# Row normalisation of a 1024 x 4096 array on one core: loads moved from the SyncE queue to the ScalarE queue

## The chip, the core and the metric

The kernel runs on one core of a Trainium2 chip. The metric is the device time of one execution in microseconds (us); lower is better. The kernel before takes 84.19 us, the median of 4 runs (84.07 to 84.33). The profile shown below was taken from one further execution, which took 84.27 us; the hardware profiler's span in it, from the first to the last instruction, is 82.5 us, so 1.8 us lie around the span.

## The reference

Each of the 1024 rows of a float32 array with 4096 columns is divided by its own length:

```python
norm = np.sqrt(np.sum(x ** 2, axis=axis, keepdims=True) + eps)
return (x / norm).astype(np.float32)
```

The axis is the last one, eps is 1e-12. 16.78 MB are read and as many are written; for every element there is one square, one addition and one multiplication.

## The kernel before, in words

The 1024 rows are cut into four tiles. A tile is 128 partitions x 2 rows (R = 2) x 4096 columns of float32; a partition holds two neighbouring rows, which are 32 KB in one piece both in memory and on the chip, and a tile is 4 MiB. The pool `io` has four buffers, as many as there are tiles, so each tile `xt` has a place of its own and no load ever waits for a buffer.

The first loop (L44 to L47) issues all four loads, one transfer per tile, with `nc.sync.dma_start` (L46): they stand in the instruction queue of SyncE (SP), one after the other, and nothing is waited for between them.

The second loop (L49 to L73) works through the tiles in order. For each tile:

- ScalarE (ACT) runs Square over the first and then the second row of every partition (L53), 128 x 4096 elements each, and accumulates the sums of squares into a column of `ssq`. The squares themselves go to one scratch tile `sq`. Each Square is followed by a short read of the accumulator. The first Square needs a table load, which stands at the head of ScalarE's instructions.
- ScalarE takes the root of the two sums plus eps (L61). The first time this needs another table load.
- VectorE (DVE) takes the reciprocal (L67) and multiplies the two rows by it, in place (L70).
- SyncE issues the store of the tile (L73), again one transfer of 4 MiB. It waits until VectorE is done with the tile.

So SyncE's instructions before are: four loads without waits, then four stores, each with its wait. Both kinds of transfer go through one queue, and a store's data stand behind those of every load that was issued before it. ScalarE issues no transfers. TensorE does nothing and GpSimd (POOL) only sets four constants. At the end (L104) every engine is drained and SyncE waits until the last store has landed.

Of the kernel before, what the change touches and what calls it, by code (L numbers as in the profile page):

```python
# [1 line left out]

# [4 lines left out]


@with_exitstack  # L10
def kernel(
    ctx: ExitStack,
    tc: tile.TileContext,
    x: bass.AP,
    axis: bass.AP,
    eps: bass.AP,
    out: bass.AP,
):
    nc = tc.nc
    P = nc.NUM_PARTITIONS  # L20

    assert isinstance(axis, int) and axis in (-1, len(x.shape) - 1)
    eps = float(eps)

    x = x.flatten_outer_dims()
    out_flat = out.flatten_outer_dims()
    N, D = x.shape
    assert N % P == 0

    R = 2  # L30
    n_tiles = N // (P * R)
    x = x.rearrange("(t p r) d -> t p (r d)", p=P, r=R)
    out_t = out_flat.rearrange("(t p r) d -> t p (r d)", p=P, r=R)

    io = ctx.enter_context(tc.tile_pool(name="io", bufs=n_tiles))
    scratch = ctx.enter_context(tc.tile_pool(name="scratch", bufs=1))
    stats = ctx.enter_context(tc.tile_pool(name="stats", bufs=4))

    sq = scratch.tile([P, D], mybir.dt.float32)
    eps_t = scratch.tile([P, 1], mybir.dt.float32)  # L40
    nc.vector.memset(eps_t, eps)  # L41

    xts = []
    for i in range(n_tiles):  # L44
        xt = io.tile([P, R, D], mybir.dt.float32)
        nc.sync.dma_start(out=xt.rearrange("p r d -> p (r d)"), in_=x[i])  # L46
        xts.append(xt)  # L47

    for i in range(n_tiles):  # L49
        xt = xts[i]  # L50
        ssq = stats.tile([P, R], mybir.dt.float32)
        for r in range(R):
            nc.scalar.activation(  # L53
                out=sq,
                in_=xt[:, r],
                func=mybir.ActivationFunctionType.Square,
                accum_out=ssq[:, r : r + 1],
            )

        rstd = stats.tile([P, R], mybir.dt.float32)  # L60
        nc.scalar.activation(  # L61
            out=rstd,
            in_=ssq,
            func=mybir.ActivationFunctionType.Sqrt,
            bias=eps_t,
        )
        nc.vector.reciprocal(out=rstd, in_=rstd)  # L67

        for r in range(R):
            nc.vector.tensor_scalar_mul(  # L70
                out=xt[:, r], in0=xt[:, r], scalar1=rstd[:, r : r + 1]
            )
        nc.sync.dma_start(out=out_t[i], in_=xt.rearrange("p r d -> p (r d)"))  # L73


# [1 line left out]
_INS = ['x', 'axis', 'eps']  # L77
_OUTS = [((1024, 4096), 'float32')]
#: Inputs that are plain numbers.
_NUMBERS = {'axis': -1, 'eps': 9.999999960041972e-13}  # L80


# [26 lines left out]
```

## Time and profile before

| What | Value |
|---|---|
| median of 4 runs | 84.19 us (84.07 to 84.33) |
| profiled execution | 84.27 us |
| its span | 82.5 us |
| DVE busy | 19.2 us (23%) |
| ACT busy | 33.4 us (41%) |
| mean traffic over the span | 407 GB/s |
| DMA packets | 1152, of which 128 under 512 B |
| share of the 16 DMA engines taken by the one queue | 96.2% |
| store issues on SP start at | 26.90, 35.33, 45.05 and 55.64 us |

How to read it: engine rows count busy time of compute instructions; instructions that only issue transfers are not counted as busy. A table by stretches gives for each stretch of the span the busy time of each engine, the number of its instructions, the granted TensorE clock, the mean busy share of the 16 DMA engines and the rate in GB/s. A packet is counted to the stretch in which it starts, so short stretches can show shares over 1. "To landing" is the time from the issue of a transfer to its last semaphore update.

### The profile page before, as it was taken

How to read it: one execution, taken by the hardware profiler on the slowest of the kernel's cores; microseconds unless marked ns; L12 is line 12 of the kernel's file. 1: busy time of each engine (PE TensorE's matmuls, PEld its weight loads, DVE VectorE, ACT ScalarE, POOL GpSimd, SP SyncE). 2: the span in 40 equal slices, each digit the busy share in tenths (PEclk: the TensorE clock that was granted, in tenths of full speed). 3: DMA queues.
4: the chain of work that ended last, by engine and by line, in shares of the span. 5: the costliest groups of instructions: out<-in, count | busy, mean ns of one | idle time of the engine just before them, and what ended most of it. 6: DMA issues, size and time to landing. Idle time of an engine off the chain costs nothing.

```text
span 82.5 us, 98 instructions
## 1 busy us (share of the span) xinstructions
DVE 19.2 (23%) x13; ACT 33.4 (41%) x22; POOL 0.2 (0%) x4
## 2 busy tenths in 40 slices
DVE  0000000000299019910498003990000000000000
ACT  6000007999699972999419996000000000000000
POOL 0000000000000000000000000000000000000000
DMA  7779997996998999899959989998998998999890
GB/s 191 302 334 445 508 429 334 508 493 302 477 508 365 397 508 445 350 477 493 270 254 508 493 350 429 509 397 365 508 445 350 477 508 350 413 508 413 350 508 0
DMA packets 1152, 33.55 MB, mean 407 GB/s; under 512 B 128, under 2 KB 128, under 8 KB 128
## 3 DMA queue, kind: packets, MB, share of 16 engines
q1 hardware_dynamic: 1152, 33.55, 96.2%
HBM read 16.78 MB, written 16.78 MB: 407 GB/s over the span
## 4 chain that ended last, share of the span: by engine, by line
DMA 50%; ACT 9%; DVE 3%; DVEq 3%; SPq 1%; issue 0%
DMA xt<-in_x_dram 50%; ACT sq L53 9%; DVE xt L70 3%; DVEq L104 3%; SPq L46 1%; ACT rstd L61 0%; DVE rstd L67 0%
## 5 line engine op out<-in xcount | busy, mean ns | idle before, releaser
L53 ACT ACTIVATE sq<-xt 128x4096 f32<-128x4096 f32 x8 | 28.9, 3617 | 16.5 <-DMA xt<-in_x_dram 16.4
L70 DVE TENSOR_SCALAR xt<-xt,rstd 128x4096 f32<-128x4096 f32 x8 | 18.5, 2350 | 0.1
L67 DVE RECIPROCAL rstd<-rstd 128x2 f32<-128x2 f32 x4 | 0.7, 166 | 35.5 <-ACT rstd L61 35.5
L53 ACT ACT_TABLE_LOAD x1 | 1.3, 1283 | 0.7 <-PEq L90 0.7
L53 ACT ACTIVATION_READ_ACCUMULATOR sq<-xt 128x1 f32 x8 | 1.5, 186 | 0.0
L61 ACT ACT_TABLE_LOAD x1 | 1.3, 1283 | 0.0
L61 ACT ACTIVATE rstd<-ssq,eps_t 128x2 f32<-128x2 f32 x4 | 1.2, 295 | 0.1
L41 DVE MEMSET eps_t<- 128x1 f32 x1 | 0.1, 59 | 0.8 <-PEq L90 0.8
L90 POOL MEMSET const-bfloat16-1.0<- 128x1 bf16 x1 | 0.1, 101 | 0.0
L90 POOL MEMSET const-uint8-127<- 128x1 uint8 x1 | 0.1, 101 | 0.0
L90 POOL MEMSET const-float32-0.0<- 128x1 f32 x1 | 0.1, 98 | 0.2 <-issue 0.2
L90 POOL MEMSET const-float32-1.0<- 128x1 f32 x1 | 0.1, 98 | 0.0
## 6 DMA issues: line engine op xcount, KB each, us to landing
xt<-in_x_dram SPq DMA_DIRECT2D x4, 4096.0 KB, 26.1
out_dram<-xt SPq DMA_DIRECT2D x4, 4096.0 KB, 26.5
```

The costliest lines, as they stand in the source:

```text
L41: nc.vector.memset(eps_t, eps)
L46: nc.sync.dma_start(out=xt.rearrange("p r d -> p (r d)"), in_=x[i])
L53: nc.scalar.activation(out=sq, in_=xt[:, r], func=mybir.ActivationFunctionType.Square, accum_out=ssq[:, r : r + 1],)
L61: nc.scalar.activation(out=rstd, in_=ssq, func=mybir.ActivationFunctionType.Sqrt, bias=eps_t,)
L67: nc.vector.reciprocal(out=rstd, in_=rstd)
L70: nc.vector.tensor_scalar_mul(out=xt[:, r], in0=xt[:, r], scalar1=rstd[:, r : r + 1])
L90: nc = _bacc.Bacc("TRN2", target_bir_lowering=False, num_devices=1)
L104: with _tile.TileContext(nc) as tc:
```

## The change

The four loads are issued with `nc.scalar.dma_start` in place of `nc.sync.dma_start`; the stores stay on SyncE. The order of the issues, the tiles and the arithmetic are the same. The pool `stats` now has `n_tiles` buffers, which is 4 as before, and the rest is names.

```diff
-    x = x.rearrange("(t p r) d -> t p (r d)", p=P, r=R)
+    x_t = x.rearrange("(t p r) d -> t p (r d)", p=P, r=R)
...
-    stats = ctx.enter_context(tc.tile_pool(name="stats", bufs=4))
+    stats = ctx.enter_context(tc.tile_pool(name="stats", bufs=n_tiles))
...
     for i in range(n_tiles):
-        xt = io.tile([P, R, D], mybir.dt.float32)
-        nc.sync.dma_start(out=xt.rearrange("p r d -> p (r d)"), in_=x[i])
+        xt = io.tile([P, R, D], F32)
+        nc.scalar.dma_start(out=xt.rearrange("p r d -> p (r d)"), in_=x_t[i])
         xts.append(xt)
```

On the engines it does this (the instruction lists of the two kernels side by side; PE, DVE and POOL are unchanged):

```
ACT: +L46 DMACopy xt<-in_x_dram 128x8192 x4     ahead of the first L53 LoadActFuncSet
SP:  -L46 DMACopy xt<-in_x_dram 128x8192 x4     ahead of the first L73 DMACopy
```

More of the change, by code (lines that the diff above doesn't have):

```diff
@@ L20 @@
     P = nc.NUM_PARTITIONS
+    F32 = mybir.dt.float32
     assert isinstance(axis, int) and axis in (-1, len(x.shape) - 1)
@@ L36 @@
     scratch = ctx.enter_context(tc.tile_pool(name="scratch", bufs=1))
-    stats = ctx.enter_context(tc.tile_pool(name="stats", bufs=4))
-    sq = scratch.tile([P, D], mybir.dt.float32)
-    eps_t = scratch.tile([P, 1], mybir.dt.float32)
+    stats = ctx.enter_context(tc.tile_pool(name="stats", bufs=n_tiles))
+    sq = scratch.tile([P, D], F32)
+    eps_t = scratch.tile([P, 1], F32)
     nc.vector.memset(eps_t, eps)
@@ L50 @@
         xt = xts[i]
-        ssq = stats.tile([P, R], mybir.dt.float32)
+        ssq = stats.tile([P, R], F32)
         for r in range(R):
@@ L58 @@
             )
-        rstd = stats.tile([P, R], mybir.dt.float32)
+        rstd = stats.tile([P, R], F32)
         nc.scalar.activation(
```

## The prediction

> **What bounds the kernel now.** I read the rows by slices first, then the table by stretches, then SP's own waits. ACT is busy 41% of the span and DVE 23%, so neither is the bound. In the table I cut the span at the moments when ACT starts on a tile (the load has just landed: 12.96, 22.68, 32.40, 42.98), and after that in stretches of 9.6 us:
>
> ```profile
> core 0: us, DVE busy (x) ACT busy (x) POOL busy (x), PEclk, DMA share, GB/s
> 0.00:2.10 2.10, 0.06 (x1) 1.28 (x1) 0.20 (x4) 1.00 0.70 187
> 2.10:12.96 10.86, 0.00 (x0) 0.00 (x0) 0.00 (x0) 1.00 0.93 398
> 12.96:22.68 9.72, 0.59 (x2) 9.00 (x7) 0.00 (x0) 1.00 1.00 432
> 22.68:32.40 9.72, 6.07 (x4) 7.71 (x6) 0.00 (x0) 1.00 1.00 432
> 32.40:42.98 10.58, 5.64 (x5) 7.71 (x5) 0.00 (x0) 1.00 1.01 396
> 42.98:52.60 9.62, 3.81 (x3) 7.71 (x5) 0.00 (x0) 1.00 1.01 436
> 52.60:62.20 9.60, 3.01 (x2) 0.00 (x0) 0.00 (x0) 1.00 1.01 437
> 62.20:71.80 9.60, 0.00 (x0) 0.00 (x0) 0.00 (x0) 1.00 1.01 437
> ```
>
> The DMA share is 0.93 to 1.01 from 2.10 on: the sixteen DMA engines are the bound, in loads (432 GB/s) as in stores (437 GB/s). One stretch stands out: the fourth load took 10.58 us where the two before it took 9.72. So 0.86 us are lost about where the loads end and the stores begin, with the engines counted as busy.
>
> The stores do not start when they are issued:
>
> ```profile
> SPq L73 <- DVE xt L70: 41.4, 4, 13.9
> SPq L104 <- DMA out_dram<-xt: 25.5, 3, 9.6
> ```
>
> ```profile
> xt<-in_x_dram SPq DMA_DIRECT2D x4, 4096.0 KB, 26.1
> out_dram<-xt SPq DMA_DIRECT2D x4, 4096.0 KB, 26.5
> ```
>
> The first store is issued at 26.90 but needs 25.7 us to land (52.6): it stands behind two loads. Singly, the four stores take 25.7, 27.0, 27.0 and 26.0 us to landing, so they land at 52.6, 62.3, 72.05 and 81.64. Each time a store is issued, other data still stand in the queue: the last one is issued at 55.64 and its turn comes only when the third is through. ACT and DVE are covered by some 15 us.
>
> **The change part by part.**
> *The issue on ACT.* Before, SP's four load issues took 1.91 us, 383 to 532 ns each, from 0.73 on. ACT's first instruction before, a table load of 1.28 us, also starts at 0.73. In the changed instruction list the four issues stand ahead of that table load, so the first load leaves at the same moment if ACT issues as fast as SP. No row shows an issue on ACT; the first one alone matters, since the engines then have 9.7 us of work. Bounds: -0.4 us (no issue time at all) to +1.28 (as late as behind the table load). I take 0, by the nearest row, SP's. The table load moves to about 2.64 and ends at 3.9; the wait for the first tile (until 12.96) hides it by 9 us. Without that cover it and the issues would cost 1.91 + 1.28 = 3.2 us. On SP the first instruction is now the wait of store 1, which stood there from 13.0 anyway; nothing else is behind the loads there. The stores keep their waits and their order, and no wait is added to an engine. `stats` had 4 buffers and has 4: nothing.
>
> *What really moves: who gets the engines from 26.9 on.* The data of both kernels are the same, 33.55 MB, and as long as the engines never run dry, the end stays where it is. So I need the time at which the last store can start, and the time at which the other seven transfers are through.
> (1) Store 1 is issued at 26.90. The first load, issued at 0.73, shows its first packets at 1.7, so I put the first store data at 27.9.
> (2) Load work left then, at the pace of 9.72 us per tile: load 3 until 32.40 and load 4 until 42.12, together 14.2 us.
> (3) Packets are all of one size (1024 of 32 KB, next to 128 small ones), and a tile of stores takes the engines as long as one of loads. No row shows two queues side by side. The stores' share lies between 0 (loads first, as now) and 1 (stores first). I take one half. The 14.2 us then become 28.4.
> (4) I keep the 0.86 us once, as a loss that is not shared: load 4 lands at 27.9 + 28.4 + 0.86 = 57.2 instead of 42.98.
> (5) From landing to store 4's issue it took 55.64 - 42.98 = 12.66 us (two Squares, the root, the reciprocal, two products, each without a gap worth naming); with 1.0 us to the first packet, store 4 can start at 57.2 + 13.7 = 70.9.
> (6) Stores 1 to 3 and all loads are done when store 3 lands, 72.05 as before. But a landing comes after its data: load 1 took 11.2 us from its first packet to its landing, 1.5 more than the pace, in which start and landing are both contained. So the engines run dry between 70.5 and 72.05.
> The 15 us of cover are used up. Taking the early end, 70.5, the engines stand empty for 0.4 us; taking the late one there is no gap at all. If the 0.86 us is doubled too, store 4 starts at 71.8 and the gap is 1.3 at most. I take **+0.3 us**, between 0 and 1.3 and near the case that counts the loss once. Stores 2 and 3 come in time: they are issued at 35.3 and, load 3 then landing at 27.9 + 2 x 4.5 = 36.9, at about 49.6, while store 1 alone lasts until 27.9 + 19.4 = 47.3 and store 2 far beyond.
>
> Sum: 84.27 (profiled) + 0 + 0.3 = 84.57. The profiled execution is 0.08 us above the median, so against the runs shown: 84.19 + 0.3 = **84.5 us**.
>
> *A rule beside the row.* The row says 432 GB/s for loads and 437 for stores, each alone. The Trainium skill, "DMA: Bandwidth & Descriptors", section "Issuing engines are not separate DMA queues", speaks against any gain: transfers issued from different engines run on the same 16 DMA engines, and only issue time is saved. By it the sum would be 84.2 or more. The same page, section "Queues, rings and completion order", has each DMA engine take turns between queues packet by packet, which would make the share one half; its section "Latency and other measured facts" lists copies with 214 GB/s per direction at full rate, which is 428 for both, and an estimate from it is 1 to 2% over some 28 us, up to 0.5 us more than my sum. No run here shows either yet.
>
> **The rivals.**
> *B, stores get more than half.* With a share s, load 4 lands at 27.9 + 14.2/(1-s) + 0.86. The gap opens when this plus 13.7 passes 70.5 to 72.05: from s = 0.49 to 0.52 on. At s = 0.55 it is 2 to 3.5 us (86 to 87.7). If stores always went first: stores 1 and 2 run until 47.3, load 3 lands at 51.8, load 4 at 62.4; store 3 can start at 65.5, 3.1 us after the engines ran dry, and store 4 at 76.1, 0.9 us after store 3: 84.2 + 4.0 = 88.2. The worst share would leave the whole 13.7 us bare (97.9). For it: the price rises at once, there is no cover left. Against: equal packets.
>
> *C, mixing costs rate.* The 0.86 us were lost where loads and stores meet. If each load packet that stands beside store packets paid a part of it, say 0.86 us per two packets: 14.2 us of loads are 14.2/(9.72/8) = 12 packets per engine, so up to 5 us: 89. Against: the stretch shows it once, and the next one is back at 436.
>
> *D, the other side: the loss at the meeting goes away.* Place: 32.40 to 42.98. Price: 0.86 us, to 83.3. If the last loads lost it because the whole stream turns from one direction to the other at one point, a stream that is mixed from 27.9 on need not turn. It decides when store 4 still starts before 70.5, that is with a share of at most one half: without the loss load 4 lands at 56.3 and store 4 can start at 70.0. For it: no other stretch lost anything. Against: mixing may as well pay it at its start.
>
> *E, the directions have limits of their own.* Then loads and stores would run side by side at full rate: load 4 still lands at about 43, store 4 is issued at 55.6 and starts at 56.7 after stores 1 to 3, and lands 10 us later, some 15 us before now: 69. Against: the share is 1.00 in one direction alone, and nothing here shows an engine doing more.
>
> *S, nothing changes*, because no engine runs dry and nothing is lost or saved: 84.2. That the change does not do what it says is out, by the instruction lists.
>
> **How the numbers follow.** About 0.2% is what a measurement of this kernel can tell from no change (84.02 to 84.36). Forecast A (a small gap, 84.4 to 85.2): 0.28. B (85.2 to 92, mostly below 88): 0.22. C (85 to 90): 0.10. D (83.0 to 84.0): 0.24. E (about 69): 0.04. S: 0.12. So slower 0.60, same 0.12, faster 0.28. The range reaches from D's low end, 83.0, to stores first, 88.2, and leaves out E and the upper parts of B and C, some 0.15. The forecast's own range is 84.4 to 85.2.
>
> **What would show it.** Step (1) to (4): ACT's start on the fourth tile, at 57 instead of 42.98; a later start, above 58.5, is B or C, and the table by stretches tells which (430 GB/s from 28 to 57 and empty slices near 70 for B; below 425 throughout for C). Step (5): store 4's issue 12.7 us after that start. Step (6): a thin slice of DMA near 70. D: no such slice, and a span near 81.6. The issue on ACT: the first tile's start at 12.96. The prediction is wrong altogether if the fourth tile still starts near 43 (loads first, or E).

## The result and the profile after

The changed kernel takes 84.45 us (median of 40 runs, 84.23 to 84.89), the kernel before in the same sessions 84.3 us (65 runs). The ratio is 1.0021, with a 95% interval of 1.0013 to 1.0029: slower by about 0.2 us. The profiled execution of the changed kernel took 84.89 us, at the upper end of its runs, with a span of 83.1 us; that of before took 84.27. The pair of profiles therefore differs by 0.6 us where the medians differ by 0.15, and only what stands out from that is read here.

First the transfers by queue, from the page of the changed kernel. There are two queues now, with half the packets each:

```profile
q10 hardware_dynamic: 576, 16.78, 49.1%
q1 hardware_dynamic: 576, 16.78, 46.8%
```

The table by stretches, cut where ScalarE starts on a tile (columns as in the prediction):

```profile
12.87:22.57 9.70, 0.58 (x2) 9.00 (x6) 0.00 (x0) 1.00 1.00 432
22.57:35.77 13.20, 8.99 (x5) 7.72 (x5) 0.00 (x0) 1.00 1.00 390
35.77:55.14 19.37, 4.78 (x3) 7.72 (x6) 0.00 (x0) 1.00 1.00 433
55.14:72.60 17.46, 4.78 (x3) 7.71 (x5) 0.00 (x0) 1.00 0.99 426
```

The reader sees three things. The first tile starts at 12.87 (12.96 before), so the issue on ScalarE costs nothing. The fourth load takes 19.37 us, twice the 9.70 of a load alone, at 433 GB/s in all: loads and stores share the engines one to one and lose no rate. And the stretch 22.57 to 35.77, in which the first store comes up, runs at 390 GB/s; against 432 that is 13.20 x (1 - 390/432) = 1.3 us lost. Before, the same reckoning for the stretch 32.40 to 42.98 at 396 GB/s gives 0.9 us.

Now around the last store, which is issued at 67.79:

```profile
66.00:69.00 3.00, 1.76 (x1) 0.00 (x0) 0.00 (x0) 1.00 0.88 382
69.00:72.00 3.00, 0.00 (x0) 0.00 (x0) 0.00 (x0) 1.00 1.14 492
72.00:75.00 3.00, 0.00 (x0) 0.00 (x0) 0.00 (x0) 1.00 0.89 382
```

Packets are counted where they start, so three neighbouring stretches scatter about 1; there is no empty one. The gap of the forecast is not there. It would be in the profile if it were: an experiment below shows how it looks.

Where the 1.3 us go can be read from one more row of the changed kernel, for the stretch from the issue of store 1 (26.80) to 30.9; the queue of the loads is q10:

```profile
DMA packets 44, 1.44 MB, mean 352 GB/s; under 512 B 0, under 2 KB 0, under 8 KB 0
## 3 DMA queue, kind: packets, MB, share of 16 engines
q10 hardware_dynamic: 44, 1.44, 103.4%
```

No store packet starts in the 4.1 us after the issue. In the next 0.4 us eight of them do. And the load packets in these 4.1 us are slow: 44 of them took 103.4% of 16 engines, 1.54 us each, where a load alone needs 16 x 9.70 / 128 = 1.21 us per packet. The kernel before has the same at the end of its fourth load, from 38.60 to 40.70, ahead of the first store packet:

```profile
DMA packets 32, 1.05 MB, mean 499 GB/s; under 512 B 0, under 2 KB 0, under 8 KB 0
q1 hardware_dynamic: 32, 1.05, 161.7%
```

That is 1.617 x 16 x 2.1 / 32 = 1.70 us each, and they are the last of the loads: up to 40.70 the queue has started 16.78 MB, all that is read. So the loss falls on the load packets just ahead of the first store packets, not on load packets that run side by side with stores.

### The profile page after: what moved, and what is told of

The parts are those of the page before. It is cut to its first block, busy times and chain, and to the rows that moved or that the text cites. A ratio compares the mean times of both kernels' runs of the same rounds, so it can differ in the third digit from the quotient of the medians.

```text
span 83.1 us, 98 instructions
## 1 busy us (share of the span) xinstructions
DVE 19.2 (23%) x13; ACT 33.4 (40%) x22; POOL 0.2 (0%) x4
## 3 DMA queue, kind: packets, MB, share of 16 engines
q10 hardware_dynamic: 576, 16.78, 49.1%
q1 hardware_dynamic: 576, 16.78, 46.8%
HBM read 16.78 MB, written 16.78 MB: 404 GB/s over the span
## 4 chain that ended last, share of the span: by engine, by line
DMA 41%; ACT 19%; another core or an unknown queue 14%; DVE 3%; DVEq 3%; ACTq 1%; issue 0%
DMA xt<-in_x_dram 41%; ACT sq L53 18%; DVE xt L70 3%; DVEq L104 3%; ACTq L46 1%; ACT rstd L61 1%; DVE rstd L67 0%
```

## The experiments

**Theory M**, formed on the two profiles: the engines never run dry (have no packets to move); what differs is a loss paid where store data first come up behind load data (the "meeting" in what follows), 0.9 us before and about 1.3 us after. **Rival G** is the forecast: a gap before the last store. **Rival P**: each load packet beside store packets pays. A fourth candidate, the issue on ScalarE, is already out by the first tile's start, and the exchange of queues tests it again. Ratios are to the kernel before, with their 95% intervals.

### Is there a gap, and how much cover is left?

The cover of the last store is the time by which it could start before the engines get to it. Three kernels lengthen the path from the landing of load 4 to the issue of store 4. Squares of the fourth tile's second row are repeated; each writes the same sum again. The lines are those of one extra Square; the other two kernels have `range(2 if i == 3 else 0)`.

```diff
+        for k in range(1 if i == 3 else 0):
+            nc.scalar.activation(
+                out=sq,
+                in_=xt[:, 1],
+                func=mybir.ActivationFunctionType.Square,
+                accum_out=ssq[:, 1:2],
+            )
```

*The kernel before with two extra Squares.*

> The kernel before with the Square of the fourth tile's second row done three times: 7.44 us more on the fourth tile's path. There store 4 is issued at 55.64 and its turn comes after 70, so every theory has it covered: 84.2 to 84.3 us, no change. If the time rises, the cover of some 15 us was misread.

Measured: 84.3 us, ratio 0.9993 (0.9972 to 1.0014). So at least these 7.4 us of the cover before are real; the rest of the 15 is read from the profile.

*The changed kernel with one extra Square.*

> The changed kernel with one Square of the fourth tile's second row done twice (the second overwrites the same sum): 3.72 us more between the landing of load 4 and the issue of store 4. Theory M: in the changed kernel store 4 is issued at 67.79, could start near 68.8, and the engines would run dry near 71.2 to 72; with 3.72 more it starts near 72.5, a gap of 0.5 to 1.3 us: 85.0 to 85.8 us. Theory G (a gap exists already): the whole 3.7 us are added, 88.1. Theory P: as M.

Measured: 85.12 us, ratio 1.0088 (1.0055 to 1.0122).

*The changed kernel with two.*

> The changed kernel with that Square done three times: 7.44 us more on the fourth tile's path. Theory M: the first 2.4 to 3.2 us are covered, the rest is bare: 84.45 + 4.2 to 5.0 = 88.7 to 89.5 us, 3.7 over the run with one extra Square. Theory G: 84.45 + 7.4 = 91.9.

Measured: 88.78 us, ratio 1.0526 (1.0481 to 1.0571). In its table by stretches (store 4 is issued at 75.66) the gap is plain:

```profile
70.00:72.00 2.00, 1.15 (x2) 0.75 (x3) 0.00 (x0) 1.00 0.57 246
72.00:74.00 2.00, 2.00 (x2) 0.00 (x0) 0.00 (x0) 1.00 0.00 0
74.00:76.00 2.00, 1.63 (x1) 0.00 (x0) 0.00 (x0) 1.00 0.00 0
76.00:78.00 2.00, 0.00 (x0) 0.00 (x0) 0.00 (x0) 1.00 1.23 524
```

The last two columns, DMA share and GB/s, are zero from 72 to 76: this is what a dry engine looks like. Of the first 3.72 us, (1.0088 - 1.0021) x 84.3 = 0.6 us reached the end; of the second 3.72, (1.0526 - 1.0088) x 84.3 = 3.7, all of it. So the changed kernel has 3.72 - 0.6 = 3.1 us of cover left (2.9 to 3.4 by the interval of the first run), where the kernel before had some 15. G falls: no gap existed.

### Does mixing cost rate?

Both kernels were run with R = 1: eight tiles of 2 MiB, packets of 16 KB, first store near 16.

```diff
-    R = 2
+    R = 1
```

> The kernel before with R = 1: eight tiles of 2 MiB, packets of 16 KB, one queue, loads first. Every theory: DMA-bound, one border between loads and stores, 84.2 to 85 us.

Measured: 84.52 us, ratio 1.0027 (1.0015 to 1.0040).

> The changed kernel with R = 1: the first store is issued near 15 instead of 26.8, so loads and stores run mixed for about 50 us instead of 27, in packets of half the size, four times as many turns between the queues. Theory M: one meeting, so within 0.5 us of the same kernel with one queue. Theory P: the cost of mixing is at least doubled (by time) or four times as large (by turns): if the 0.6 us by which the profiled spans differ is such a cost, 1.2 to 2.4 us over the same kernel with one queue. Theory G: the last tile's path is only about 6.6 us here, so no gap.

Measured: 84.62 us, ratio 1.0054 (1.0030 to 1.0077). The intervals of the two overlap. The stretches of the two-queue kernel between tile starts show why it is no more:

```profile
16.30:26.05 9.75, 5.05 (x5) 5.33 (x7) 0.00 (x0) 1.00 1.01 403
26.05:35.78 9.73, 2.52 (x2) 4.00 (x3) 0.00 (x0) 1.00 1.01 433
35.78:45.52 9.74, 2.52 (x2) 4.00 (x3) 0.00 (x0) 1.00 1.01 431
45.52:55.23 9.71, 2.52 (x2) 4.00 (x3) 0.00 (x0) 1.00 1.01 432
55.23:64.96 9.73, 2.52 (x2) 4.01 (x4) 0.00 (x0) 1.00 1.01 431
```

Each load takes twice its 4.9 us and the sum of both directions stays at 431 to 433 GB/s for 39 us of mixing. Only the first stretch, where they meet, is low: 403. P falls; what is lost is lost at the meeting.

### Is the loss paid at every meeting?

One queue, as before, with load 4 moved behind store 1: load, load, load, store, load, store, store, store.

```diff
-        nc.sync.dma_start(out=xt.rearrange("p r d -> p (r d)"), in_=x[i])
+        if i < 3:
+            nc.sync.dma_start(out=xt.rearrange("p r d -> p (r d)"), in_=x[i])
...
         nc.sync.dma_start(out=out_t[i], in_=xt.rearrange("p r d -> p (r d)"))
+        if i == 0:
+            nc.sync.dma_start(out=xts[3].rearrange("p r d -> p (r d)"), in_=x[3])
```

> One queue (SyncE) as before, but the fourth load stands behind the first store, so the single queue runs loads 1 to 3, store 1, load 4, stores 2 to 4: it meets a store after a load twice instead of once. Theory M (the loss of about 0.9 us is paid where store data come up behind load data, and no engine runs dry): one more meeting, 84.2 + 0.9 = 85.1 us, and the third load, not the fourth, is the first to land late (33.3 instead of 32.4). Theory G (what moves the time is a gap before the last store): the fourth load lands near 53, store 4 is issued near 65.5 with stores 2 and 3 still to run, no gap, 84.2 us. Theory P (each load packet beside store packets pays): two borders instead of one, 84.2 + 0.9 too, so P is not told from M here.

Measured: 84.55 us, ratio 1.0007 (0.9984 to 1.0029). The 0.9 us that M gave to a second meeting are outside the interval, which ends at 0.25 us over before (84.37 us in the same session). So M as stated falls. The stretches between its tile starts:

```profile
22.90:33.53 10.63, 7.00 (x5) 7.71 (x5) 0.00 (x0) 1.00 1.01 395
33.53:43.30 9.77, 3.92 (x3) 7.72 (x5) 0.00 (x0) 1.00 0.99 429
43.30:53.13 9.83, 2.86 (x2) 0.00 (x1) 0.00 (x0) 1.00 1.01 437
```

Now the third load is the late one: 10.63 us, as the fourth was before (10.58). From there on store 1 and load 4 take 19.6 us together, 0.2 more than twice 9.7, and the rate is 429 and 437. The loss moves with the first meeting and is paid once. That is theory **M'**. Its rival **L**: the stores need this time to start up, wherever they come, also where no load is in their way.

### Without a meeting

A small copy of 512 bytes from a tile stands ahead of the stores on SyncE and holds them until that tile's load has landed. The first kernel takes `xts[2]` in place of `xts[3]`.

```diff
+    held = scratch.tile([1, 128], F32)
+    nc.sync.dma_start(out=held, in_=xts[3][0:1, 0, 0:128])
```

*Held to the third load* (two queues):

> The changed kernel with one small copy (512 bytes of the third tile to a scratch tile) ahead of the stores on SyncE: it waits until the third load has landed, so the first store is issued near 33 instead of 26.8. The meeting then falls into load 4 and the mixed time shrinks from 27 to about 20 us. Theory M: the cost of the meeting is the same, load 4 lands near 52, no gap: 84.3 to 84.5 us. Theory P: a quarter less mixing, a quarter of the cost of mixing gone; as the changed kernel is only 0.2% over before, that is under 0.1 us, so P speaks here only through the place of the loss: spread over the mixed time, not at its start.

Measured: 84.35 us, ratio 1.0016 (0.9998 to 1.0035). It lies between before and after, and tells neither from the other. The time was as expected, the course was not: store 1 is issued at 33.05, but no store packet starts before 39.4, so that load 4 lands already at 46.34, not near 52, and loads and stores run mixed for some 7 us, not 20.

*Held to the fourth load* (two queues):

> The changed kernel with the small copy taken from the fourth tile: the stores are issued only when the last load has landed, so loads and stores never meet. Theory M: the fourth load lands after 9.7 us, near 42.0 instead of 42.98 in the kernel before, since the late landing there comes from store data behind it; then the engines stand empty from the last load data to the first store data, about 0.5 us before the landing plus some 1.3 us for the copy's and the store's issue and start: 84.2 - 0.9 + 1.8 = 85.1 us (84.6 to 85.8). If the fourth load still lands near 42.9, the late landing has nothing to do with the stores, and the time is near 86.

Measured: 85.97 us, ratio 1.0209 (1.0191 to 1.0228), 0.9 over M's 85.1 and beyond its range; the time is the one named for the other case, so the landing has to decide. The line at which ScalarE starts on the fourth tile, and the stretches around it:

```profile
42.09 3.62 ACT L56 ACTIVATE sq<-xt 128x4096 f32<-128x4096 f32 x1 [1.94 <-DMA xt<-in_x_dram]
```

```profile
32.37:42.10 9.73, 4.80 (x4) 7.73 (x6) 0.00 (x0) 1.00 0.87 377
42.10:43.80 1.70, 1.70 (x2) 1.70 (x1) 0.00 (x0) 1.00 0.01 0
```

The fourth load lands at 42.09, 9.72 us after the third: the lateness is gone with the stores behind it, so it was theirs. The same stretch as above, 38.60 to 40.70, has the same 32 packets of 32 KB, now at the usual 1.21 us each:

```profile
DMA packets 32, 1.05 MB, mean 499 GB/s; under 512 B 0, under 2 KB 0, under 8 KB 0
q10 hardware_dynamic: 32, 1.05, 115.5%
```

The price is larger than I reckoned: store 1 is issued only at 42.78, after the copy, and the engines are empty to 43.8, and for some time before 42.1 as well (377 GB/s in that stretch). From that I took the remedy: release the stores some 2.5 us before the last load is through.

*Held to three quarters of the fourth load.* Load 4 is issued as two transfers, of 6144 and 2048 of its 8192 columns; the copy reads the first part. The other three loads stay whole.

```diff
+            nc.scalar.dma_start(out=flat[:, :6144], in_=x_t[i][:, :6144])
+            nc.scalar.dma_start(out=flat[:, 6144:], in_=x_t[i][:, 6144:])
```

> Two queues, as in the changed kernel, but load 4 is cut into a first part of three quarters and a last one of a quarter (2.4 us of engine time), and the small copy that holds the stores waits for the first part. With the stores held to the full landing, the engines stood empty for some 2.5 us; here the first store data should come up just as the last load data run out, near 41.5. Theory M' (the loss of 0.7 to 1.4 us is paid once, when store data first come up while load data are still being served; later turns are free): neither the loss nor the gap, load 4 lands at 42.1, 84.3 - 0.9 + 0 to 0.3 = 83.4 to 83.7 us, under both kernels. Rival theory L (the first store data need that time wherever they come, as a start-up of the store direction): 84.3 to 84.5, no gain.

Measured: 83.76 us, ratio 0.9936 (0.9919 to 0.9953): just above the range of M', well under that of L.

*The same on one queue*, everything on SyncE:

> The same hold and the same cut of load 4, but all transfers on the SyncE queue as in the kernel before. M': the number of queues does not matter, as loads and stores do not meet: 83.4 to 83.7 us, as with two queues. L: 84.3 to 84.5. If two queues cost something by themselves, this kernel is faster than the one with two queues by 0.2 us.

Measured: 83.84 us, ratio 0.9941 (0.9924 to 0.9959). Two queues or one: no difference that can be told.

*Held to five eighths* (two queues, parts of 5120 and 3072 columns):

> As the two-queue kernel with the quarter, but the last part of load 4 is three eighths (3.6 us), so that the first store data come up about 1.2 us, one packet per engine, before the last load data have gone. M': a part of the loss comes back, 83.7 to 84.1 us, between the quarter and the changed kernel. L: 84.3 to 84.5.

Measured: 83.47 us, ratio 0.9901 (0.9885 to 0.9917): faster than both kernels, by 0.8 us than before. I had expected part of the loss to come back here, and it did not; the quarter was too short. The stretches between landings in this kernel:

```profile
32.29:42.06 9.77, 4.83 (x4) 9.71 (x6) 0.00 (x0) 1.00 1.04 445
42.06:51.78 9.72, 6.83 (x5) 5.61 (x5) 0.00 (x0) 1.00 1.00 432
51.78:61.43 9.65, 0.81 (x1) 0.00 (x0) 0.00 (x0) 1.00 1.01 435
```

Load 4 lands after 9.77 us and store 1 another 9.72 us later, without a late tile and without an empty stretch. L falls: the stores can start at no loss. What the three held kernels do not separate is the time of release from the smaller last packets: a partition of load 4 ends in a piece of 12 or 8 KB here, not 32 KB, and the cut alone, without the hold, was not run.

### The queues exchanged

Loads on SyncE, stores on ScalarE, where their waits stand among the Squares.

```diff
-        nc.scalar.dma_start(out=xt.rearrange("p r d -> p (r d)"), in_=x_t[i])
+        nc.sync.dma_start(out=xt.rearrange("p r d -> p (r d)"), in_=x_t[i])
...
-        nc.sync.dma_start(out=out_t[i], in_=xt.rearrange("p r d -> p (r d)"))
+        nc.scalar.dma_start(out=out_t[i], in_=xt.rearrange("p r d -> p (r d)"))
```

> Queues exchanged: loads on SyncE, stores on ScalarE, where a store's issue stands among the Squares and waits for VectorE. The first store is issued near 27 as before and the two queues share the engines the same way. M': 84.3 to 84.6 us, as the changed kernel, if the ScalarE instructions held up behind the store issues stay under the 3 us of cover that the changed kernel has left; the fourth tile starts near 55. If ScalarE's own issue of the loads costs anything, this kernel is at 84.2 to 84.3 like the kernel before.

Measured: 84.55 us, ratio 1.0028 (1.0011 to 1.0044), as the changed kernel. The fourth tile starts at 54.96 and store 4 is issued at 67.62, within 0.2 us of the changed kernel. So the 0.2% do not come from ScalarE issuing the loads.

## Why the prediction was right, and where it was not

The direction held, and the size: 0.3 us forecast, 0.15 to 0.18 us measured (1.0021 x 84.3). The term that made the sign, however, was the wrong one: the gap, put at 0.3, is 0. That the number came close is luck.

**The issue on ACT** at 0: right (12.87 against 12.96; the exchange of queues agrees).

**The share of one half**: right. The fourth load took 19.37 us where 2 x 9.70 was reckoned. The rule drawn on in the prediction, that the engines take turns packet by packet (the Trainium skill, "DMA: Bandwidth & Descriptors", "Queues, rings and completion order"), agrees with that row. The estimate from that page's 214 GB/s per direction (428 for both, listed for copies between HBM tensors) does not: the mixed stretches run at 431 to 433.

**Step (1)**, first store data at 27.9: wrong by 3 us. I took the 1.0 us from issue to first packet from an idle moment at the start of the span; with the loads' queue full, no store packet starts before 30.9. The kernel with the queues exchanged has the same: store 1 is issued at 26.88, and no store packet starts before 31.1. Fewer store packets then get ahead of load 4: it lands at 55.14, not the 57.2 of **step (4)**, although the loss that step (4) counts at 0.86 is about 1.3.

**Step (5)**: 67.79 - 55.14 = 12.65 us from landing to issue, as reckoned. Store 4 can start near 68.8 instead of 70.9.

**Step (6)** failed as the source of the gap. I took the early end, 70.5, for the moment at which the engines run dry. The added Squares put it at about 68.8 + 3.1 = 71.9, the late end. With both corrections the cover is 3.1 us instead of -0.4, the gap term is 0, and what remains of the sum is the case S.

**What makes the 0.2%.** The gap, the rate of mixing and the issuing engine are out. Left is the first meeting, 1.3 us against 0.9 in the one pair of profiles. But its size differs from execution to execution: the same reckoning gives 0.6 to 1.3 us in the profiles of five kernels with two queues (the changed one, its two with added Squares, the one held to the third load, the exchanged one) and 0.6 to 0.9 in three with one queue (before, with added Squares, with load 4 behind store 1), so the pair alone decides nothing. With stores that hardly meet the loads, one and two queues are alike (0.9941 and 0.9936); where they do meet, both kernels with two queues from 27 on lie above before (1.0021 and 1.0028), and the one-queue kernel that meets as early is at 1.0007. That would fit a meeting that costs some 0.2 us more between two queues than within one. But the intervals overlap, and by the medians of its session (84.55 against 84.37) the one-queue kernel is 0.2 us over before as well, so it is not shown; the cause of the 0.2% stays open.

**The rivals.** B: the share was one half, and the point from which it would decide lies higher than I put it, as 3.1 us were to spare. C is refuted by the R = 1 pair and the mixed rates. D is right in what it says of the loss and wrong in the remedy: the 0.86 us can be had, but the change does not avoid the meeting, it moves it from 39 to 30. The held kernels avoid it, and the best of them reaches 83.47, where D put 83.3. E is refuted by 433 GB/s for both directions together.

## What to carry to other kernels

Here the DMA engines were the bound and never ran dry, and moving transfers between queues hardly changed the sum of their work (0.2%); it spent cover. The cover of the last store fell from some 15 us to 3.1, and compute added on that path beyond these 3.1 us was paid in full (3.7 of the second 3.72). Price such a change by the moment when the last transfer can start against the moment when the others end, and take the delay from issue to first data from a loaded moment, not from the start of the span. Look for the stretch in which a busy engine moves less than elsewhere: that 0.9 us, not the queue, was what could be had here, by cutting the last load and releasing the first store just as the loads run out.

## What the runs showed that was not expected

- A store issued into the second queue, while the first holds loads, showed its first packet after more than 4.1 us (26.80 to 30.9; 4.2 with the queues exchanged, over 6 when held to the third load), against 1.0 us for the first load of an idle core.
- The first time store data come up behind load data, 0.9 to 1.3 us of the engines' time are lost in the two kernels, with the engines counted as busy: the load packets just ahead of the first store packets take 1.5 to 1.7 us instead of 1.21. No second loss of this size came with a second turn from loads to stores in the same queue (1.0007, 0.9984 to 1.0029). Why these packets are slow, no row shows.
- If the last load is cut and the stores are held so that their data come as its last 12 KB pieces go, the loss does not occur: 83.47 us, 0.9901 of before. With whole loads and the stores held to the last landing it does not occur either, but the empty engines then cost more (85.97 us).
- Loads and stores mixed run at 431 to 433 GB/s together, the rate of either alone, in packets of 32 KB and of 16 KB alike.
